# A layer with a 32-expert mixture streamed from HBM: expert order, a ninth gate/up buffer, an in-place residual, down chunks in 8 KB pieces

## The chip, the cores and the metric

The kernel runs on one core of one Trainium2 chip. The metric is the device time of one execution in microseconds (us). Engine names in the profile: PE is the matrix engine, PEld its weight loads, DVE the vector engine, ACT the scalar engine, POOL the GpSimd engine, SP the sync engine, on whose queue nearly all loads are issued.

## What is computed

One layer on 256 tokens of 1024 channels, everything in float32. First a token-mixing part (a convolution branch and a spatial gating branch, merged and projected). Then layer norm, and a mixture of 32 experts in which every token uses the four experts with the highest router logits. An expert is a gated unit of width 1024:

```python
gate, up = jnp.split(xb @ w_gu[e] + b_gu[e], 2, axis=-1)
gate = jnp.minimum(gate, SWIGLU_LIMIT)
up = jnp.clip(up, -SWIGLU_LIMIT, SWIGLU_LIMIT)
act = (up + 1) * (gate * jax.nn.sigmoid(SWIGLU_ALPHA * gate))
return act @ w_dn[e] + b_dn[e]
```

Its results are weighted by the softmax of the four logits, summed per token, multiplied by a gate vector g2 (made from the conditioning input), added to 2^(1/4) times the residual, and normed. The weights `w_gu` are 8 MiB per expert and `w_dn` 4 MiB.

## The kernel before

The token mixer comes first; its weights pass through five tiles `raw` of 1 MiB and are split into high and low parts in tiles `hi` and `lo`. Routing follows: the top four of each token, the tokens per expert, and the experts sorted by their number of tokens. Expert 0 is always worked first, since its weights can be loaded before the routing is known; the other places of the list `KINDS` (line 32) are filled by rank.

The expert stage is a list of 30 jobs, one expert each, written out by hand. The kind of a job says how many tokens it has room for (`CAP`): W 192, A 128, B 64, C 32. A "wide" job (W, A) feeds PE 128 columns of tokens; B puts two groups of 64 columns of the PE array side by side and C four groups of 32, so that a chunk of weights needs fewer passes. W is an A and a B at once. A float32 product appears in the profile as two passes (two MATMUL instructions). Experts with more tokens than their place has room for would be finished by tail jobs at the end, each under a condition; with these inputs none is run.

A job needs 12 chunks of weights of 1 MiB: 8 gate/up chunks (128 rows of `w_gu`, 8 KB per partition) and 4 down chunks (256 rows of `w_dn`; partition p holds rows p and 128 + p, two pieces of 4 KB). Loads are issued on SP's queue in the order in which the buffers come round: gate/up chunks through `N_G` = 7 buffers, the five `raw` tiles and two of a pool `rawx`, and down chunks through `N_D` = 4 buffers of `rawx`. The pool `rawx` lies where `hi` and `lo` were. `next_gu` and `next_dn` issue the next load right after the product that read the buffer's last content; a load waits on the queue until the buffer is free, and what is behind it on the queue waits too.

The order on PE, from the main loop (line 1371 on): the gate/up products of job j, then the down products of job j - 1. Smaller pieces of work are put between the chunks from a list `waiting`, one step per chunk (`tick`, `begin`): the gather of the next batch of jobs' tokens (`BATCHES`, at most 256 columns each, line 948), the transposes of the gate/up result (line 1208), the activation on DVE and ACT (lines 1176 to 1196), the slot weights (lines 1104, 1105), and the scatter of finished outputs into the result `y` (lines 1334, 1342). `until` runs steps from the list until a condition holds. An output tile `ob` (`N_OB` = 3) is taken by a wide job or by two narrow ones together, and given back at its scatter.

The result `y` has a tile of its own in the pool `a8` (seven slots of 8 KB per partition, shared with the gathered inputs `S`, the down bias, W's extra tile `wx` and the routed tokens); `start_units` sets it to the weighted down bias times g2 plus the scaled residual `x1`.

Column c of the gate/up result sits in block c // 128, so that the transposed activations of a block lie on 128 partitions, in the order in which the rows of `w_dn` are loaded.

Of the kernel before, what the change touches and what calls it, by code (L numbers as in the profile page):

```python
# [9 lines left out]
F32 = mybir.dt.float32  # L10
# [4 lines left out]
ALU = mybir.AluOpType  # L15
# [13 lines left out]

KINDS = ("B", "B", "A", "C", "C", "W", "C", "C", "A", "C", "C", "B", "B", "A", "C", "C", "A", "C", "C",
         "B", "B", "B", "B", "C", "C", "A", "C", "C", "C", "C")
CAP = {"W": 192, "A": 128, "B": 64, "C": 32}
RANK0 = {"W": 1, "A": 2, "B": 7, "C": 14}
BATCHES = ((0, 1, 2), (3, 4, 5), (6, 7, 8, 9, 10), (11, 12, 13), (14, 15, 16, 17, 18), (19, 20, 21, 22),
           (23, 24, 25, 26, 27), (28, 29))
NSTATIC = len(KINDS)
COLS = [j + sum(k == "W" for k in KINDS[:j]) for j in range(NSTATIC)]
NV = COLS[-1] + 1  # L40
# [19 lines left out]
NAT_O = (0,)  # L60
AHEAD = 2
N_RAW, N_HI, N_LO = 5, 9, 6
N_G, N_D = 7, 4
N_OB = 3
K_NORM = 5
C_M1 = 2.26
END0 = True
# [8 lines left out]
def kernel(ctx, tc, a, out):  # L76
# [114 lines left out]
    def load_gu(col, k, raw):  # L191
# [4 lines left out]
        sp.dma_start(raw, src)  # L196
        return raw

    def load_dn(col, ci, raw):
        if col == 0:  # L200
            src = a["w_dn"][0, 0, ci * 256:(ci + 1) * 256].rearrange("(k p) c -> p k c", p=P)
        else:
            src = a["w_dn"][0, ds(expert_reg(col), 1), ci * 256:(ci + 1) * 256].rearrange("o (k p) c -> p (o k) c", p=P)
        sp.dma_start(raw.rearrange("p (k c) -> p k c", k=2), src)
        return raw

    def next_gu():
        m = count["xg"]
        count["xg"] += 1
        if m < NSTATIC * KC:  # L210
            raw = raw_x("xg", N_G - N_RAW) if m % N_G < N_G - N_RAW else raw_tile()
            ring_g.append(load_gu(COLS[m // KC], m % KC, raw))

    def next_dn():
# [499 lines left out]
    rawx.append(ctx.enter_context(tc.tile_pool(name="rawx", bufs=1, side="right")))  # L714
    bgr = yap.tile([E, 2 * D], F32, name="bgr", tag="ya")
    sp.dma_start(bgr, a["b_gu"][0])
    for i in range(N_G):
        next_gu()
    for i in range(N_D):
        next_dn()  # L720
# [181 lines left out]
    for t in range(NT):  # L902
        ve.tensor_tensor(P1[:, t], pj[:, t * 64:t * 64 + NV], first_tok, op=ALU.add)
    g2_step(100)

    mix.close()
    tmp = ctx.enter_context(tc.tile_pool(name="tmp", bufs=2))
# [103 lines left out]
    base_q = const.tile([P, NTAIL], F32, name="base_q")  # L1011
    tgt_q = const.tile([P, NTAIL], F32, name="tgt_q")
    P1q = const.tile([P, NT, NTAIL], F32, name="P1q")
    bcols = const.tile([P, 2 * KC, NJOB], F32, name="bcols")

    def tail_unit():

# [39 lines left out]
                                        op0=ALU.add, op1=ALU.subtract)  # L1057
        return [counts, starts, places]

    def bias_unit(h):  # L1060

        box = []

        def mm():
            box.append(MS())
            for c in range(KC):
                pe.matmul(box[0][:, c * 64:c * 64 + NJOB], lhsT=bgr[:, (h * KC + c) * P:(h * KC + c + 1) * P],
                          rhs=J[:, 0:NJOB], start=True, stop=True)

        def out_():  # L1070
            ve.tensor_scalar(bcols[:, h * KC:(h + 1) * KC], box[0].rearrange("p (c j) -> p c j", c=KC)[:, :, 0:NJOB],
                             float(h), None, op0=ALU.add)
        return [mm, out_]

    def weight_unit():
# [17 lines left out]

    bdn = A8([E, D], name="bdn")
    gp.dma_start(bdn, a["b_dn"][0])
    y = A8([P, NT, D], name="y")

    def slot_weights(key, lhs_r, lhs_f, target, store):

# [74 lines left out]
    def swiglu_in(gv, uv, bg, bu, shape):  # L1174
        r = "p (c s) -> p c s" if len(shape) == 3 else "p (c h s) -> p c h s"
        kw = {"c": shape[1]} if len(shape) == 3 else {"c": shape[1], "h": shape[2]}
        n = 1
        for x in shape[1:]:
            n *= x
        gt = tmp.tile([P, 512], F32, name=nm("gt"), tag="gt", bufs=2)[:, 0:n]  # L1180
        ut = tmp.tile([P, 512], F32, name=nm("ut"), tag="ut", bufs=1)[:, 0:n]
        ve.tensor_tensor(gt.rearrange(r, **kw), gv, bg.to_broadcast(shape), op=ALU.add)  # L1182
        ve.tensor_scalar(gt, gt, 7.0, None, op0=ALU.min)
        sc.activation(gt, gt, AF.Silu, scale=SW_A)
        ve.tensor_tensor(ut.rearrange(r, **kw), uv, bu.to_broadcast(shape), op=ALU.add)
        ve.tensor_scalar(ut, ut, 8.0, -6.0, op0=ALU.min, op1=ALU.max)
        return gt.rearrange(r, **kw), ut.rearrange(r, **kw)

    def act_units(job):

        us = []
        col = job.col
        job.left = {"W": 4, "A": 2, "B": 2, "C": 1}[job.kind]

        def done(dst, gu):
# [9 lines left out]

        def transposes(ps, g, blocks):
            for i, c in enumerate(blocks):
                pe.transpose(ps[:, i * P:(i + 1) * P], g[:, c * P:(c + 1) * P], ident)  # L1208

        def bias(part, hh):  # L1210
            k0 = part * KC + hh * 4
# [137 lines left out]
    def start_units():  # L1349

        def unit(t, n):
            box = []

            def mm():
                box.append(MS())
                pe.matmul(box[0], lhsT=combT[:, t * P:(t + 1) * P], rhs=bdn[:, n * 512:(n + 1) * 512],
                          start=True, stop=True)
            ns = slice(n * 512, (n + 1) * 512)

            def out_():  # L1360
                ve.tensor_tensor(y[:, t, ns], box[0], g2c[:, ns], op=ALU.mult)
                ve.scalar_tensor_tensor(y[:, t, ns], x1[:, t, ns], ALPHA, y[:, t, ns], op0=ALU.mult, op1=ALU.add)
            return [mm, out_]
        return [unit(t, n) for t in range(NT) for n in range(2)]

# [70 lines left out]
    def tail_job(q):  # L1436
# [4 lines left out]
        for kk in range(KC // 2):  # L1441
            ps = MS()
            gather_mm(ps, St, kk, oht, P)
            gather_out(St, ps, kk, P)
        gu_open(job)
        for k in range(KC):
            gu_mm(job, k, load_gu(job.col, k, raw_tile()))
# [56 lines left out]
```

## Time and profile before

| what | value |
|---|---|
| three runs, lowest, median, highest | 1271.09, 1273.22, 1273.25 us |
| profiled execution, its span | 1268.86 us, 1267.0 us |
| PE busy | 1123.8 us (89%) |
| PEld busy | 548.3 us (43%) |
| DVE busy | 484.7 us (38%) |
| ACT busy | 205.7 us (16%) |
| read from HBM, mean rate over the span | 446.92 MB, 354 GB/s |
| gate/up loads | 240 of 1 MiB |
| down loads | 120 of 1 MiB |
| mean granted clock of TensorE | 0.954 |

The page divides the span into 40 slices and gives for each the busy share of the engines and the rate of the transfers. The ends of matrix instructions are modelled, so a busy PE is not one at its peak, and two passes that follow each other overlap in the record: the difference of two starts is the better measure of what a pass takes. A wait on SP's queue names what the next load waited for.

### The profile page before, as it was taken

Reading aid. Unit: us, or ns where it says so; the run is one execution under the profiler, and the core shown is the slowest. Engines: PE = TensorE matmul, PEld = TensorE weight load, DVE = VectorE, ACT = ScalarE, POOL = GpSimd, SP = SyncE. Lnnn points to the kernel's source line nnn. Section 1 sums busy time; section 2 is a strip of 40 time slices with the busy share of each in tenths; the row PEclk is TensorE's granted clock in tenths of the full one; section 3 lists DMA queues with packets and bytes.
Section 4 is the critical chain, followed back from the end, with each engine's and each line's share of the span. In section 5 each row is a group of like instructions: output and inputs, shape, how many; then the busy total and the mean of one; then the engine's idle time right before and its main releaser. Section 6 shows DMA issues by size and latency. Waiting matters only on the chain. (4 is left out here: it accounts for less than half of the span.)

```text
span 1267.0 us, 14367 instructions
## 1 busy us (share of the span) xinstructions
PE 1123.8 (89%) x5454; PEld 548.3 (43%) x5454; DVE 484.7 (38%) x926; ACT 205.7 (16%) x344; POOL 55.5 (4%) x185
## 2 busy tenths in 40 slices
PE   1999999998999989999997999899888986998672
PEld 1998898876434334324331343334222321332110
DVE  6799999976321410321222113121121211132124
ACT  1533234533202001000110020011000100011000
POOL 6000000000200001000010010000000000000000
PEclk9999999999999999999998999899889988999676
DMA  9984346685897998999999999999999999999993
GB/s 367 368 334 134 116 151 223 231 306 204 349 418 293 383 418 330 375 399 404 377 417 417 417 403 404 416 417 416 416 417 417 416 417 418 417 417 417 417 414 111
DMA packets 84312, 449.13 MB, mean 354 GB/s; under 512 B 7377, under 2 KB 7417, under 8 KB 51424
## 3 DMA queue, kind: packets, MB, share of 16 engines
q1 hardware_dynamic: 82672, 443.84, 87.8%
q0 software_dynamic: 1552, 4.15, 0.9%
q8 instruction: 50, 0.82, 0.3%
q14 instruction: 38, 0.31, 0.1%
HBM read 446.92 MB, written 1.05 MB: 354 GB/s over the span
## 5 line engine op out<-in xcount | busy, mean ns | idle before, releaser
L1138 PE MATMUL big<-raw,S 128*32 128x512 f32 (+1 forms) x1600 | 279.0, 631 | 30.3 <-DMA raw<-in_w_gu_dram 30.3
L1149 PE MATMUL big<-raw,S 128*128 128x512 f32 x384 | 172.2, 602 | 0.0
L1314 DVE TENSOR_TENSOR ob<-big,g2c 64x512 f32<-64x512 f32 x48 | 33.0, 688 | 361.8 <-PE big L1289 253.1
L1138 PEld LDWEIGHTS big<-raw,S 128*32 128x32 f32 (+1 forms) x1600 | 63.3, 122 | 202.7 <-issue 128.8
L1149 PEld LDWEIGHTS big<-raw,S 128*128 128x128 f32 x384 | 71.9, 192 | 90.4 <-issue 89.3
L1289 PE MATMUL big<-raw,aT 128*32 128x512 f32 x512 | 75.9, 706 | 30.5 <-DMA raw<-in_w_dn_dram 29.2
L516 DVE SCALAR_TENSOR_TENSOR sg<-ya,par,sg 128x256 f32<-128x256 f32 x240 | 100.0, 470 | 0.6
L1280 PE MATMUL big<-raw,aT 128*128 128x512 f32 x192 | 87.0, 601 | 0.9 <-DMA raw<-in_w_dn_dram 0.9
L426 PE MATMUL big<-hT,raw 128*128 128x256 f32 x384 | 85.5, 379 | 0.0
L1342 PE MATMUL ms<-ob,ohT 128*128 128x512 f32 x144 | 76.8, 640 | 5.9 <-DVE gt L1182 3.2
L1334 DVE TENSOR_TENSOR y<-y,ms 128x512 f32<-128x512 f32 x72 | 48.9, 685 | 81.8 <-PE ms L1342 81.7
L426 PEld LDWEIGHTS big<-hT,raw 128*128 128x128 f32 x384 | 71.9, 190 | 9.5 <-issue 0.5
L1138 PE MATMUL big<-raw,aT 128*64 128x512 f32 x256 | 65.1, 621 | 4.2 <-DMA raw<-in_w_dn_dram 4.1
L147 DVE TENSOR_TENSOR lo<-raw,hi 128x1024 fp32r<-128x1024 f32 x46 | 55.2, 1216 | 9.5 <-ACT hi L146 6.4
L1172 ACT COPY g<-big 128x512 f32<-128x512 f32 x16 | 9.4, 585 | 302.1 <-PE big L1138 302.1
L1280 PEld LDWEIGHTS big<-raw,aT 128*128 128x128 f32 x192 | 35.2, 190 | 52.4 <-issue 50.6
L146 ACT CAST hi<-raw 128x1024 fp32r<-128x1024 f32 x46 | 46.3, 1051 | 59.1 <-DMA raw<-in_w_in_dram 17.3
L430 PE MATMUL big<-hThi,lo 128*128 128x256 f32 x192 | 55.0, 288 | 0.8 <-DVE lo L147 0.8
L428 PE MATMUL big<-hThi,hi 128*128 128x256 f32 x192 | 55.7, 291 | 0.0
L429 PE MATMUL big<-hTlo,hi 128*128 128x256 f32 x192 | 55.0, 287 | 0.1
L1289 PEld LDWEIGHTS big<-raw,aT 128*32 128x32 f32 x512 | 13.9, 118 | 87.5 <-DMA raw<-in_w_dn_dram 59.3
L1182 DVE TENSOR_TENSOR gt<-ms,bcols 128x256 f32<-128x256 f32 (+1 forms) x46 | 22.6, 491 | 75.0 <-PE ms L1208 75.0
(327 smaller groups left out, 1185.5 us busy)
## 6 DMA issues: line engine op xcount, KB each, us to landing
raw<-in_w_gu_dram SPq DMA_DIRECT2D x240, 1024.0 KB, 17.2
raw<-in_w_dn_dram SPq DMA_DIRECT2D x120, 1024.0 KB, 16.6
raw<-in_w_mod_dram SPq DMA_DIRECT2D x24, 1024.0 KB, 7.6
raw<-in_w_in_dram SPq DMA_DIRECT2D x24, 1024.0 KB, 7.1
raw<-in_w_b_dram SPq DMA_DIRECT2D x4, 1024.0 KB, 5.0
raw<-in_w_a_dram SPq DMA_DIRECT2D x4, 1024.0 KB, 5.0
raw<-in_w_out_dram SPq DMA_DIRECT2D x4, 1024.0 KB, 9.0
x<-in_x_dram SPq DMA_DIRECT2D x1, 1024.0 KB, 8.3
```

The source lines that it names most:

```text
L147: ve.tensor_tensor(c.lo[q], src, f(c.hi[q]), op=ALU.subtract)
L426: pe.matmul(o, lhsT=ck.raw[:, k2 * D + n * P:k2 * D + (n + 1) * P], rhs=af[:, k], start=b0, stop=b1)
L428: pe.matmul(o, lhsT=ck.hi[k2][:, s], rhs=ahi[:, k], start=b0, stop=False)
L429: pe.matmul(o, lhsT=ck.hi[k2][:, s], rhs=alo[:, k], start=False, stop=False)
L430: pe.matmul(o, lhsT=ck.lo[k2][:, s], rhs=ahi[:, k], start=False, stop=b1)
L516: ve.scalar_tensor_tensor(cT[:, n], ya[:, n, t:t + T], bcol(n, t), cT[:, n], op0=ALU.mult, op1=ALU.add)
L1138: pe.matmul(out_[q * n:(q + 1) * n], lhsT=S, rhs=raw[:, w0(q):w0(q) + 512], start=first_, stop=last_)
L1149: pe.matmul(job.ps[h][:, n * 512:(n + 1) * 512], lhsT=S[:, k, 0:P], rhs=raw[:, h * D + n * 512:h * D + (n + 1) * 512], start=f0, stop=f1)
L1280: pe.matmul(job.pd[0][:, n * 512:(n + 1) * 512], lhsT=job.aT[:, k, 0:P], rhs=raw[:, k2 * D + n * 512:k2 * D + (n + 1) * 512], start=f0, st ...
L1289: pe.matmul(job.pd[0][q * 32:(q + 1) * 32, 0:512], lhsT=job.aT[:, k, 0:32], rhs=raw[:, k2 * D + h * 512:k2 * D + (h + 1) * 512], start=ci ...
L1334: ve.tensor_tensor(yy, yy, box[0], op=ALU.add)
L1342: pe.matmul(box[0], lhsT=w()[r, t * P:(t + 1) * P], rhs=o(n)[r], start=i == 0, stop=i == len(parts_) - 1)
```

## The change

- `KINDS` has the same 30 jobs in another order: W goes from the sixth place to the twenty-third, the first A from the third to the fifth, behind B B C C. `BATCHES` is cut anew to fit (still at most 256 columns a batch).
- `N_G` goes from 7 to 9. Of nine buffers in turn, the first five are `raw` tiles, the next three come from `rawx`, and the ninth from the pool `a8`. Before routing, the eight gate/up chunks of expert 0 are asked for; the ninth load, the second job's first, is issued after the routing result.
- The residual grows in place: `y` is the tile `x1` itself. `start_units` puts the bias product into a scratch tile and adds it to the scaled residual in `x1`.
- Down chunks: partition p now holds rows 2p and 2p + 1 of the 256, which lie together in memory: one piece of 8 KB. The transposed activations have to come in that order too, so block c of the gate/up result, and of the gate/up bias, is now every second column of a stretch of 256 (`chans`).
- Other sizes: two output tiles instead of three, one scratch tile `gt` instead of two, and bias columns for the 31 columns of the list and one tail job, which is filled when a tail job runs.

```diff
-KINDS = ("B", "B", "A", "C", "C", "W", "C", "C", "A", "C", "C", "B", "B", "A", "C", "C", "A", "C", "C",
-         "B", "B", "B", "B", "C", "C", "A", "C", "C", "C", "C")
+KINDS = ("B", "B", "C", "C", "A", "C", "C", "B", "B", "A", "C", "C", "A", "B", "B", "B", "B", "C", "C",
+         "A", "C", "C", "W", "C", "C", "A", "C", "C", "C", "C")
...
-BATCHES = ((0, 1, 2), (3, 4, 5), (6, 7, 8, 9, 10), (11, 12, 13), (14, 15, 16, 17, 18), (19, 20, 21, 22),
-           (23, 24, 25, 26, 27), (28, 29))
+BATCHES = ((0, 1, 2, 3), (4, 5, 6, 7), (8, 9, 10, 11), (12, 13, 14), (15, 16, 17, 18), (19, 20, 21), (22, 23, 24),
+           (25, 26, 27, 28, 29))
...
-N_G, N_D = 7, 4
-N_OB = 3
+N_G, N_D = 9, 4
+N_OB = 2
...
+    def chans(c):
+        c0 = c // 2 * 256 + c % 2
+        return slice(c0, c0 + 255, 2)
...
-            src = a["w_dn"][0, ds(expert_reg(col), 1), ci * 256:(ci + 1) * 256].rearrange("o (k p) c -> p (o k) c", p=P)
-        sp.dma_start(raw.rearrange("p (k c) -> p k c", k=2), src)
+            src = a["w_dn"][0, ds(expert_reg(col), 1), ci * 256:(ci + 1) * 256].rearrange("o (p k) c -> p (o k c)", k=2)
+        sp.dma_start(raw, src)
...
-            raw = raw_x("xg", N_G - N_RAW) if m % N_G < N_G - N_RAW else raw_tile()
+            i = m % N_G
+            raw = raw_tile() if i < N_RAW else raw_x("xg", N_G - 1 - N_RAW) if i < N_G - 1 else A8([P, 2 * D], name="raw")
...
-    for i in range(N_G):
+    for i in range(min(N_G, KC)):
         next_gu()
...
     g2_step(100)
+    for i in range(KC, N_G):
+        next_gu()
...
-    bcols = const.tile([P, 2 * KC, NJOB], F32, name="bcols")
+    bcols = const.tile([P, 2 * KC, NV + 1], F32, name="bcols")
...
-                pe.matmul(box[0][:, c * 64:c * 64 + NJOB], lhsT=bgr[:, (h * KC + c) * P:(h * KC + c + 1) * P],
-                          rhs=J[:, 0:NJOB], start=True, stop=True)
+                pe.matmul(box[0][:, c * 64:c * 64 + w], lhsT=src[:, chans(h * KC + c)],
+                          rhs=J[:, c0:c0 + w], start=True, stop=True)
...
-    y = A8([P, NT, D], name="y")
+    y = x1
...
-        gt = tmp.tile([P, 512], F32, name=nm("gt"), tag="gt", bufs=2)[:, 0:n]
+        gt = tmp.tile([P, 512], F32, name=nm("gt"), tag="gt", bufs=1)[:, 0:n]
...
-                pe.transpose(ps[:, i * P:(i + 1) * P], g[:, c * P:(c + 1) * P], ident)
+                pe.transpose(ps[:, i * P:(i + 1) * P], g[:, chans(c)], ident)
...
-                ve.tensor_tensor(y[:, t, ns], box[0], g2c[:, ns], op=ALU.mult)
-                ve.scalar_tensor_tensor(y[:, t, ns], x1[:, t, ns], ALPHA, y[:, t, ns], op0=ALU.mult, op1=ALU.add)
+                gb = tmp.tile([P, 512], F32, name=nm("gt"), tag="gt", bufs=1)
+                ve.tensor_tensor(gb, box[0], g2c[:, ns], op=ALU.mult)
+                ve.scalar_tensor_tensor(y[:, t, ns], y[:, t, ns], ALPHA, gb, op0=ALU.mult, op1=ALU.add)
```

## Rows read from the trace of the kernel before

**Rows 1.** The page's part 2, 40 slices of 31.7 us each, the rate of all transfers.

```profile
GB/s 367 368 334 134 116 151 223 231 306 204 349 418 293 383 418 330 375 399 404 377 417 417 417 403 404 416 417 416 416 417 417 416 417 418 417 417 417 417 414 111
```

**Rows 2.** Windows, expert stage: us; busy PE, PEld, DVE, ACT, POOL; PEclk; DMA; GB/s.

```profile
322.00:1240.00 918.00, 831.62 (x3685) 298.33 (x3683) 198.87 (x414) 90.28 (x166) 22.05 (x59) 0.95 0.99 402
```

**Rows 3.** The same view, gate/up chunks alone, then down chunks alone.

```profile
1198.00:1210.00 12.00, 10.30 (x35) 2.88 (x28) 4.62 (x10) 1.00 (x2) 0.00 (x0) 0.60 1.02 421
1216.50:1226.30 9.80, 6.44 (x34) 0.77 (x32) 0.00 (x0) 0.00 (x0) 0.00 (x0) 0.65 1.02 410
```

**Rows 4.** The same view in windows of 20 us, four of ten.

```profile
380.00:400.00 20.00, 20.00 (x78) 10.84 (x77) 1.77 (x5) 4.43 (x9) 1.78 (x4) 1.00 0.93 358
400.00:420.00 20.00, 20.00 (x97) 7.23 (x98) 8.64 (x15) 3.67 (x5) 1.26 (x4) 1.00 0.70 279
...
500.00:520.00 20.00, 20.00 (x132) 7.53 (x129) 8.71 (x18) 5.10 (x7) 0.30 (x2) 1.00 0.70 260
...
780.00:800.00 20.00, 19.65 (x97) 6.40 (x99) 5.62 (x11) 1.00 (x2) 0.00 (x0) 1.00 0.99 396
```

**Rows 5.** Waits of the sync queue, 322 to 1240 us: total us, times, longest.

```profile
SPq L196 <- PE big L1138: 255.9, 112, 13.5
```

**Rows 6.** Gate/up loads (L196), 340 to 1220 us: issue to landing.

```profile
DMA to landing us min/median/max: 4.7/17.5/21.2
```

**Rows 7.** PE in order of time, 455 to 545 us: start, us, operation, count.

```profile
460.38 3.60 PE L1149 MATMUL big<-raw,S 128*128 128x512 f32 x8
463.91 1.94 PE L1138 MATMUL big<-raw,S 128*64 128x512 f32 x8
465.78 3.70 PE L1149 MATMUL big<-raw,S 128*128 128x512 f32 x8
...
488.36 0.50 PE L948 MATMUL ms<-oh,hnhi 128*128 128x256 f32 x2
...
489.41 3.60 PE L1149 MATMUL big<-raw,S 128*128 128x512 f32 x8
...
507.50 3.64 PE L1289 MATMUL big<-raw,aT 128*32 128x512 f32 x32
...
512.95 1.92 PE L1138 MATMUL big<-raw,S 128*32 128x512 f32 x16
514.81 1.09 PE L1208 MATMUL ms<-ident,g 128*128 128x128 f32 x8
...
519.76 1.04 PE L1342 MATMUL ms<-ob,ohT 128*128 128x512 f32 x2
520.73 1.07 PE L1138 MATMUL big<-raw,S 128*32 128x512 f32 x8
...
523.88 1.88 PE L1280 MATMUL big<-raw,aT 128*128 128x512 f32 x4
...
526.70 1.98 PE L1280 MATMUL big<-raw,aT 128*128 128x512 f32 x4
```

**Rows 8.** PE in order of time, 405 to 445 us: A's down chunks.

```profile
423.82 13.14 PE L1280 MATMUL big<-raw,aT 128*128 128x512 f32 x30
```

**Rows 9.** PE's groups by line and shape, 322 to 1241 us (busy us, mean ns).

```profile
L1208 PE MATMUL ms<-ident,g 128*128 128x128 f32 x224 | 36.7, 293 | 15.7 <-ACT g L1172 7.6 <-ACT g L1170 7.0 <-DVE gt L1182 1.0
```

**Rows 10.** The sync queue in order of time, 255 to 345 us.

```profile
274.91 20.96 SPq L196 DMA_DIRECT2D raw<-in_w_gu_dram  x4
295.90 0.43 SPq L204 DMA_DIRECT2D raw<-in_w_dn_dram  x1
302.80 0.33 SPq L196 DMA_DIRECT2D raw<-in_w_gu_dram  x1
303.17 0.43 SPq L204 DMA_DIRECT2D raw<-in_w_dn_dram  x1
311.18 6.96 SPq L196 DMA_DIRECT2D raw<-in_w_gu_dram  x2
```

**Rows 11.** All engines in order of time, 1228 to 1270 us.

```profile
1240.87 1.06 PE L1289 MATMUL big<-raw,aT 128*32 128x512 f32 x8 [1.10 <-DMA raw<-in_w_dn_dram]
```

More of the change, by code (lines that the diff above doesn't have):

```diff
@@ L197, in load_gu @@
         return raw
+    def chans(c):
+        c0 = c // 2 * 256 + c % 2
+        return slice(c0, c0 + 255, 2)
     def load_dn(col, ci, raw):
         if col == 0:
-            src = a["w_dn"][0, 0, ci * 256:(ci + 1) * 256].rearrange("(k p) c -> p k c", p=P)
+            src = a["w_dn"][0, 0, ci * 256:(ci + 1) * 256].rearrange("(p k) c -> p (k c)", k=2)
         else:
-            src = a["w_dn"][0, ds(expert_reg(col), 1), ci * 256:(ci + 1) * 256].rearrange("o (k p) c -> p (o k) c", p=P)
-        sp.dma_start(raw.rearrange("p (k c) -> p k c", k=2), src)
+            src = a["w_dn"][0, ds(expert_reg(col), 1), ci * 256:(ci + 1) * 256].rearrange("o (p k) c -> p (o k c)", k=2)
+        sp.dma_start(raw, src)
         return raw
@@ L1058, in tail_unit, with bias_unit @@
         return [counts, starts, places]
-    def bias_unit(h):
+    def bias_unit(h, src=bgr, c0=0, dst=0, n=NV, w=NV):
         box = []
@@ L1066, in mm @@
             for c in range(KC):
-                pe.matmul(box[0][:, c * 64:c * 64 + NJOB], lhsT=bgr[:, (h * KC + c) * P:(h * KC + c + 1) * P],
-                          rhs=J[:, 0:NJOB], start=True, stop=True)
+                pe.matmul(box[0][:, c * 64:c * 64 + w], lhsT=src[:, chans(h * KC + c)],
+                          rhs=J[:, c0:c0 + w], start=True, stop=True)
         def out_():
-            ve.tensor_scalar(bcols[:, h * KC:(h + 1) * KC], box[0].rearrange("p (c j) -> p c j", c=KC)[:, :, 0:NJOB],
-                             float(h), None, op0=ALU.add)
+            ve.tensor_scalar(bcols[:, h * KC:(h + 1) * KC, dst:dst + n],
+                             box[0].rearrange("p (c j) -> p c j", c=KC)[:, :, 0:n], float(h), None, op0=ALU.add)
         return [mm, out_]
@@ L1191, in act_units @@
         us = []
-        col = job.col
+        col = NV if job.tail else job.col
         job.left = {"W": 4, "A": 2, "B": 2, "C": 1}[job.kind]
@@ L1444, in tail_job @@
             gather_out(St, ps, kk, P)
+        br_ = raw_tile()[:E]
+        sp.dma_start(br_, a["b_gu"][0])
+        waiting.extend(bias_unit(h, br_, job.col, NV, 1, 8) for h in range(2))
+        flush()
         gu_open(job)
```

## The prediction

> **What bounds the kernel now.** I read the page's slices first [rows 1]. From the twelfth slice on the transfers run at 417 GB/s nearly everywhere; the slices well below that (293, 330, 375) all lie in the first half of the expert stage. In the slices before it the token mixer runs, at 116 to 368 GB/s, and the transfers are not the limit. So in the expert stage (322 us to 1240 us) the bound is the weight stream: 30 experts of 12 chunks of 1 MiB. The window over that stage [rows 2] shows 402 GB/s over 918 us with PE busy for 832 us of it.
>
> Next, what the stream could do. In a stretch where only gate/up chunks are moving the rate is 421 GB/s, in one with only down chunks 410 GB/s [rows 3]. 1,048,576 bytes divided by these is 2.49 us and 2.56 us per chunk. Two gate/up chunks to one down chunk give 417.4 GB/s, so the stage lost (1 - 402/417.4) x 918 = 33.9 us to holes in the stream.
>
> Then where the holes are. From 360 us on ten windows of 20 us lie below 400 GB/s, of which [rows 4] shows four, the first and the last among them; each window's hole is (417.4 - rate)/417.4 x 20 us. Those from 380 to 440 us hold 11.9 us (2.8 and 6.6 of it in the two shown), those from 480 to 520 us 9.8 us (7.5 in 500:520), the other five, up to 780:800, 7.7 us. Together 29.4 us; the remaining 4.5 us are single late transfers and the start. In the windows of the holes PE is busy without a pause: there PE is the limit.
>
> Last, why. The sync queue issues loads in order and each needs a free buffer; its longest waits in sum are for PE to finish reading [rows 5]. A load takes between 4.7 us and 21.2 us to land [rows 6]: 4.7 us when the stream is empty (2.2 us of start beside the 2.49), and about 20 us, eight chunks, when PE is the one that waits.
>
> **What each expert asks of PE.** Pitches are read as differences of starts. W's gate chunk is a wide part of 3.5 us (460.38 to 463.91) and a 64-row part of 1.87 us (463.91 to 465.78) [rows 7]. So A costs 3.5 us per gate chunk (28 us) and the same per down chunk (13.1 us for 30 of the 32 passes [rows 8], 14 us), C 0.93 us per gate chunk (16 passes from 512.95 to 514.81) and 3.64 us for all its down chunks [rows 7], B 1.87 us for each of 12 chunks, W 5.4 us per gate chunk and 2.82 us for each half of a down chunk (523.88 to 526.70; 22.6 us). Each part's scatter is four products of about 1.0 us (519.76 to 520.73); two narrow experts share one. A transpose takes 0.13 us (8 in 1.09 us from 514.81 on). Slot weights add some 0.3 us to a narrow expert, 0.7 us per wide part, and a batch's gather 4 us (four units like 488.36 to 489.41). Sums: A 28 + 14 + 2 + 4 + 1 = 49 us, B 22.4 + 1 + 2 + 0.3 = 26, C 7.4 + 3.6 + 0.5 + 2 + 0.3 = 14, W 43.2 + 22.6 + 3 + 8 + 1.4 = 78. The 12 chunks of an expert take the stream 30.2 us. So A puts PE 19 us behind and W 48 us; B gives back 4 and C 16. In total 5 x 49 + 8 x 26 + 16 x 14 + 78 + 8 x 4 = 787 us: PE has time enough, only not where it is needed.
>
> **The order.** Before, the stage opens B B A: at its start every buffer is full, two B's give back 8 us, A takes 19, and the stream stands still from 380 us on. Then C C W: PE starts W with the stream about 20 us deep in queued loads; W's gate stage runs 47.1 us (460.38 to 507.50 [rows 7]); the stream lives on 20 + 8 x 2.49 = 39.9 us, so it is dry for 7.2 us, plus one restart of 2.2 us: 9.4 us, and the windows gave 9.8 us. The rule holds, so I apply it to the new order. B B C C gives back 8 + 32 us, more than the full buffers (11 to 13 chunks, 27 to 32 us), so the first A starts with PE waiting for data: its 28 us and some 3 us of transposes and scatter are less than 39.9, no hole. Each A C C asks 49 + 28 + 4 = 81 us of PE against 90 of the stream, so the later A's start the same way. W C C asks 78 + 28 + 4 = 110 us against 90.
>
> **Nine buffers.** Two more gate/up buffers are 5 us of stream. W's gate stage loses the gather it now shares (three units, 2.8 us, as W is no longer the last of its batch) and gains four transposes: about 45 us against 39.9 + 5 = 44.9, no hole to speak of. Behind W C C PE owes 20 us, and A's gate stage adds 31 - 20 = 11: 31 us against 13 chunks less the two being read, 27 us. That leaves 4 us and a restart of 2.2: 6 us of holes, all at the A after W. Bounds: none, if the C's run at their pace with full clock, and 18 us, what A and W together have now. With the 4.5 us of stray ones: 10.5 us against 33.9, **-23.4 us**.
>
> **Down chunks in 8 KB pieces.** The rows of a gate/up chunk are 8 KB already, and the move makes the two layouts equal, so I take the gate/up rate [rows 3]: 119 chunks x (2.557 - 2.491) us = **-7.9 us**; the other end is 0. The Trainium skill's "DMA: Bandwidth & Descriptors" (Specifications) gives 512 B as the least piece for line rate; by that rule 4 KB pieces lose nothing and this term is 0, against a difference of 2.7% in the rows.
>
> **The strided transposes this needs.** The same channels now sit at stride two in the copied gate tile, for the 224 + 8 transposes at L1208 and the bias products. No row shows PE reading at a stride. Lower end: nothing. Upper end: by the nearest row, the contiguous transpose [rows 7, 9], a doubling is 232 x 0.13 = 30 us more PE work, 1 us per expert, of which only that in W, the A after it and the C's between them (some 5 us) is uncovered; elsewhere PE waits for data anyway. I take 0. The Trainium skill's "SBUF — State Buffer" (Door 1: The DMA port swizzle) says that fp32 reads may skip within a 16-byte line at no cost, which would be this case; no run here shows it.
>
> **The start.** Before routing only expert 0 can be loaded. Before, four gate/up loads went out from 274.91 to 295.87 us, a down load at 295.90, and then one or two each time a chunk of the gate vector was used up; the ninth went out at about 317.8 us (the second of the pair from 311.18 on) and, with 4.7 us in an empty stream, landed at about 322.5 [rows 10]. Now there are eight gate/up loads instead of seven ahead of the four down loads, the raw tiles are filled first, and the ninth comes after the routing result. I expect the third new buffer to take the place of the first down load in the queue at 295 us: again nine landed by 322.5 us, **0 us**. Bounds: if the raw tiles block the queue until their chunks are free (302.80, 311.18, 317.8), four fewer have landed, +10 us; if all of the space opens at 295 us, two more, -5 us. The queue behind a blocked load is only other loads; PE starts expert 0 at 320 us in either case, as its gather sets that.
>
> **What costs nothing.** The ninth buffer lives in the seven slots shared with the gathered inputs, W's extra tile and the down bias; the separate result tile leaves that pool as the residual takes its place, so at most seven are live, as before. It is loaded when its own last reader is done. Cover gone, 26 loads would each pay up to a restart of 2.2 us, 57 us. Two output tiles instead of three: an output waits for the scatter one expert earlier, which is in PE's order before it; forced early it is the same work, 0 to 1 us per A. One gate scratch tile: its uses follow one another on DVE already. The in-place residual has as many instructions as before. The tail code isn't run. After the last landing nothing changes: the last down product at 1240.87 us [rows 11] is followed by 26.1 us of scatter, branches, norm and output.
>
> **Sum.** The profiled span is 1267.0 us, the execution 1268.86. -23.4 - 7.9 = -31.3 us: 1237.6 us for that execution. The median of the runs shown lies 4.36 us above it, so 1241.9 us, **1242 us**.
>
> **Rivals.** (1) *The pieces bring nothing* (the lower rate of the down stretches comes from something else in them): 1250 us. For it: nothing in the rows but that only two kinds of stretches are compared. (2) *The raw tiles block the queue at the start*: 1252 us. For it: these loads did hold up down loads behind them [rows 10]. (3) *The two buffers don't reach the stream*, since no more than eight chunks are in flight (21.2 us at most [rows 6]): W's hole stays at 5 + 2.2 us, 1249 us. Against it: a landed chunk that waits for PE is also a lead. (4) *Nothing is left at the A after W and more lands early*: 6 + 5 us less, 1231 us; with one of them about 1236 us. (5) Slower: *the strided reads make PE the bound.* Place: L1208. At five times the price PE's 787 us grow by 232 x 0.52 = 121 to 908 us; its waits for copies, first data and uneven order (832 busy and 86 idle of the 918 us, of which some 40 remain) bring that to 948 us, 30 us over the 918 us of now: 1273 + 30 = 1303 us. It decides from about four times the price on (787 + 40 + 91 = 918); at three times there is still a gain. For it: only that no row shows such a read.
>
> **How the numbers follow.** Forecast 0.54; (1) 0.12, (2) 0.10, (3) 0.10, (4) 0.08, (5) 0.04, and 0.02 for no change by several of these at once. Forecast's own spread is holes of 4.5 to 22.5 us: 1236 to 1254 us. Adding (1) to (3) in part, one with another and a doubled transpose (+6): up to 1260; (4) sets the lower end: 1231 to 1260 us. A measurement of this kernel can't tell less than 0.2% from no change. Every case but the last two is faster by more: 0.94 faster, 0.02 same, 0.04 slower.
>
> **What would show it.** The windows from 380 to 520 us at 417 GB/s or more, those with only down chunks at 421; a dip only some 740 us into the stage, at the A behind W; nine chunks landed at 322.5 us; the last down product about 1210 us; L1208's mean near 0.29 us as now [rows 9]. Wrong if the dips come with every ninth load, if transposes are several times longer, or if the first window after 322 us is starved.

## The result, and the profile after

The changed kernel takes 1256.24 us (median; 1253.1 to 1257.74, 4 runs) against 1272.15 us in the same session: ratio 0.988, interval 0.986 to 0.9896. That is faster by 1.2%, clear of the noise, inside the range, and 14 us above the predicted 1242. The profiled execution went from 1268.86 to 1257.14 us where 1237.6 was forecast: it is 19.5 us short.

Two rows of PE divide this. The first product of an expert started at 320.30 us before and at 326.98 us after; the last down chunk's product, which follows the last landing, at 1240.87 [rows 11] and 1229.13 us. So the start lost 6.7 us, the stage between them went from 920.6 to 902.1 us (31.3 less was forecast, 18.4 came: 12.9 short), and the tail, from that product to the end of the span, is 25.9 us (26.1 before). After, PE in order of time at both ends:

```profile
326.98 1.94 PE L1147 MATMUL big<-raw,S 128*64 128x512 f32 x8
...
1229.13 1.06 PE L1298 MATMUL big<-raw,aT 128*32 128x512 f32 x8 [1.07 <-DMA raw<-in_w_dn_dram]
```

The slices of the page after, beside [rows 1], each 31.4 us. From the twelfth to the thirty-first they lie at 418 to 420 GB/s; then come four of 396, 305, 390 and, two further on, 352. The holes of the first half are gone; there are new ones around W and the A behind it, which now stand late.

```profile
GB/s 365 366 317 165 102 132 237 180 330 196 311 420 419 419 420 419 418 420 420 420 420 419 419 420 419 419 419 419 420 420 419 396 305 390 417 352 419 418 406 119
```

Windows after, beside [rows 2, 4]: the stage, three places that were dips before, and W's gate stage and the A's behind it.

```profile
329.00:1229.00 900.00, 823.40 (x3683) 302.76 (x3681) 200.63 (x414) 90.82 (x166) 21.84 (x57) 0.96 1.00 410
380.00:400.00 20.00, 17.59 (x115) 6.69 (x114) 5.41 (x13) 1.80 (x4) 0.28 (x1) 1.00 1.01 421
400.00:420.00 20.00, 11.34 (x75) 1.83 (x73) 0.00 (x0) 2.42 (x5) 0.00 (x0) 0.82 1.01 419
500.00:520.00 20.00, 15.84 (x104) 5.46 (x98) 3.69 (x8) 2.93 (x6) 0.00 (x0) 1.00 1.01 419
980.00:1000.00 20.00, 20.00 (x62) 6.85 (x60) 0.48 (x1) 0.38 (x1) 0.28 (x1) 1.00 0.97 402
1000.00:1020.00 20.00, 20.00 (x82) 6.83 (x84) 0.00 (x0) 3.04 (x3) 0.00 (x0) 1.00 0.61 216
1100.00:1120.00 20.00, 20.00 (x82) 8.19 (x80) 0.00 (x0) 2.02 (x2) 0.00 (x0) 1.00 0.83 311
```

In the quiet windows PE is busy for 11 to 18 of 20 us and the transfers run without a gap: there the stream is the limit. In the last three PE is busy throughout, and the stream falls to 402, 216 and 311 GB/s. The sync queue's waits from 322 to 1240 us say the same: its largest are now for the transfers themselves. Those of gate/up loads for the narrow products fell from 255.9 us [rows 5] to 132.7, those for the wide parts of W and A from 114.0 to 50.8. Before, then after:

```profile
SPq L196 <- PE big L1149: 114.0, 34, 12.0
```

```profile
SPq L196 <- DMA raw<-in_w_gu_dram: 143.1, 76, 2.9
SPq L196 <- PE big L1147: 132.7, 72, 10.6
...
SPq L196 <- PE big L1158: 50.8, 17, 5.1
```

Holes can also be counted by the landings of the 360 loads: the time between two landings, less 2.491 us a chunk, or 2.557 us for a down chunk of before; whatever is over 0.3 us, behind the ninth landing. So counted they were 35.1 us before and are 23.4 us after.

### The profile page after: what moved, and what is told of

Read it like the earlier page. It is cut to its first block, busy times and chain, and to the rows that moved or that the text cites. A ratio compares the mean times of both kernels' runs of the same rounds, so it can differ in the third digit from the quotient of the medians.

```text
span 1255.0 us, 14491 instructions
## 1 busy us (share of the span) xinstructions
PE 1122.0 (89%) x5454; PEld 558.4 (44%) x5454; DVE 486.9 (39%) x928; ACT 206.1 (16%) x344; POOL 51.4 (4%) x183
## 5 line engine op out<-in xcount | busy, mean ns | idle before, releaser
L1147 PE MATMUL big<-raw,S 128*32 128x512 f32 (+1 forms) x1600 | 275.0, 623 | 22.4 <-DMA raw<-in_w_gu_dram 22.4
L1343 DVE TENSOR_TENSOR x<-x,ms 128x512 f32<-128x512 f32 x72 | 49.3, 686 | 188.8 <-PE ms L1351 188.5
L1298 PE MATMUL big<-raw,aT 128*32 128x512 f32 x512 | 82.0, 730 | 28.8 <-DMA raw<-in_w_dn_dram 24.5
L1193 ACT ACTIVATE gt<-gt 128x256 f32<-128x256 f32 (+1 forms) x46 | 21.7, 472 | 334.7 <-DVE gt L1192 334.7
L1147 PE MATMUL big<-raw,aT 128*64 128x512 f32 x256 | 57.9, 596 | 0.7 <-DMA raw<-in_w_dn_dram 0.7
L1217 PEld LDWEIGHTS ms<-ident,g 128*128 128x128 f32 x224 | 32.2, 208 | 57.0 <-issue 23.4
L1217 PE MATMUL ms<-ident,g 128*128 128x128 f32 x224 | 40.5, 314 | 18.7 <-ACT g L1181 7.3
L1289 PEld LDWEIGHTS big<-raw,aT 128*128 128x128 f32 x192 | 35.8, 190 | 45.1 <-issue 44.9
```

The lines of the kernel that those rows point to most:

```text
L1147: pe.matmul(out_[q * n:(q + 1) * n], lhsT=S, rhs=raw[:, w0(q):w0(q) + 512], start=first_, stop=last_)
L1217: pe.transpose(ps[:, i * P:(i + 1) * P], g[:, chans(c)], ident)
L1289: pe.matmul(job.pd[0][:, n * 512:(n + 1) * 512], lhsT=job.aT[:, k, 0:P], rhs=raw[:, k2 * D + n * 512:k2 * D + (n + 1) * 512], start=f0, st ...
L1298: pe.matmul(job.pd[0][q * 32:(q + 1) * 32, 0:512], lhsT=job.aT[:, k, 0:32], rhs=raw[:, k2 * D + h * 512:k2 * D + (h + 1) * 512], start=ci ...
```

## The experiments

The stage is the last down chunk's start less the first expert product's, from each run's profile; the time is the median. Differences are in us against the kernel before in the same session. A profile is of one execution, which can lie some microseconds off the median: that of the pieces alone took 1271.81 us, 4.2 above it, that of the order alone 1264.26, 3.3 below, that of the late A with 192 bytes 1241.21, 3.0 below.

| kernel | first product | stage | median | to before | ratio, interval |
|---|---|---|---|---|---|
| before | 320.3 | 920.6 | 1272.15 | | |
| changed | 327.0 | 902.1 | 1256.24 | -15.9 | 0.9878 [0.986, 0.9896] |
| order alone | 321.2 | 915.1 | 1267.58 | -4.2 | 0.9968 [0.9946, 0.9991] |
| pieces alone | 324.1 | 919.7 | 1267.62 | -4.1 | 0.996 [0.9939, 0.9981] |
| all but the order | 326.5 | 913.2 | 1267.22 | -4.5 | 0.9963 [0.9944, 0.9983] |
| changed, again | 326.8 | 900.8 | 1255.71 | -16.0 | 0.9859 [0.983, 0.9889] |
| late A | 325.2 | 895.7 | 1250.11 | -22.5 | 0.9826 [0.9803, 0.985] |
| seven buffers | 325.5 | 917.0 | 1271.71 | -0.9 | 0.9995 [0.9976, 1.0013] |
| seven, tiles moved back | 321.3 | 915.0 | 1265.64 | -6.9 | 0.9955 [0.9935, 0.9975] |
| 4 KB pieces | 325.4 | 909.4 | 1263.40 | -9.2 | 0.9926 [0.9899, 0.9953] |
| late A, batches recut | 325.1 | 901.8 | 1258.58 | -12.6 | 0.989 [0.9866, 0.9915] |
| late A, 192 bytes | 320.0 | 893.0 | 1244.26 | -26.9 | 0.9773 [0.9748, 0.9797] |
| before, 64 bytes | 324.5 | 922.8 | 1277.33 | +6.1 | 1.004 [1.0021, 1.0058] |
| late A, 64 bytes | 324.7 | 894.8 | 1247.31 | -23.9 | 0.9804 [0.9774, 0.9834] |

**The parts one at a time.** The first runs take the change apart. The order alone, in the kernel before (KINDS and BATCHES of the diff, nothing else):

> The kernel before with the new order of jobs and batches alone (seven buffers, 4 KB pieces, own result tile). Holes theory (what PE cannot do in the time the buffers bridge is lost to the stream, wherever it falls): the dips from 380 to 520 us go, W's gate stage at about 965 us leaves a hole of some 16 us (50.8 us of PE work against 20 + 8 x 2.49 = 39.9 us, and two restarts of 2.2), the A behind it about 8: 24 + strays 4.5 against 34, so 5 to 10 us faster than before, about 1264 us. Rival (the order alone is the whole gain): 16 us faster, 1256 us. Rival (the late start belongs to the change): first expert product at 320 us here, 327 us in the full change.

The pieces alone, in the kernel before (chans(), load_dn, the bias products and the transposes of the diff, nothing else):

> The kernel before with down chunks in 8 KB pieces and the strided transposes alone. Holes theory: 2.49 us instead of 2.56 us a down chunk, 7.9 us less stream, of which about 2 us come back as longer holes where PE is behind: 5 to 7 us faster, about 1266 us; a window with only down chunks reads 421 GB/s. Rival (strided reads cost as much as they bring): no change, 1272 us, transposes at twice their 0.13 us.

All but the order: the changed kernel with KINDS and BATCHES of before:

> The changed kernel with the order and batches of before: nine buffers, 8 KB pieces, in-place residual. Holes theory: the pieces' 6 us and two chunks more (5 us each at the A in the third place, at W and at the A's behind it): 14 to 21 us faster than before, 1251 to 1258 us, as fast as the full change or faster. Rival (the order is the whole gain): 6 us faster, 1266 us. If the ninth buffer or the third xg buffer makes the start late, the first expert product is at 327 us here too; if the start only differs between executions, it may be anywhere from 320 to 327 us.

And the changed kernel once more:

> The changed kernel unchanged, profiled again. If its late start (first expert product at 326.98 us against 320.3 us before, with the same code ahead of it) is the change's, it is within 1 us of 327 again; if it differs from execution to execution, it lies elsewhere between 319 and 328 us. The holes at W and the A behind it are there again, 16 us within 1.

Order and pieces bring some 4 us each by themselves, nine buffers with pieces in the old order 4.5, and all of them 16. So they don't add up. (Nine buffers alone were not run, and the start takes part of it: 326.5 us in all but the order, 324.1 with the pieces.) The traces show why. With seven buffers and the old order PE is what the stream waits for: with pieces alone the down chunks land 0.066 us earlier each and the holes grow from 35.1 to 42.8 us, so that in the profiled execution what is saved on the way is given back at the next wide expert. With the order alone the early holes close, and those at W and A reappear from 1000 us on (29.7 us in all). Pieces alone, then the order alone:

```profile
400.00:420.00 20.00, 20.00 (x96) 8.38 (x94) 3.62 (x7) 4.96 (x8) 3.04 (x7) 1.00 0.62 242
```

```profile
1000.00:1020.00 20.00, 20.00 (x114) 7.46 (x116) 4.97 (x9) 3.67 (x4) 0.00 (x0) 1.00 0.78 295
```

Two forecasts of these runs failed. A hole of 16 us was expected at W with the order alone; the landings give 4.7 to 5.7 us, since W's gate stage took 44.0 us there (967.08 to 1011.07) and not the 50.8 of the changed kernel. And 14 to 21 us were expected of all but the order; 4.5 came, with holes of 34.3 us against the 42.8 of the pieces alone, and 13.0 of them at W (landings from 507.9 to 520.5 us), whose gate stage took 52.3 us there (463.33 to 515.63): PE's order puts three units of a gather and three down chunks of the expert ahead into it.

**Seven buffers in the new order.**

```
-N_G, N_D = 9, 4
+N_G, N_D = 7, 4
```

> The changed kernel with seven gate/up buffers instead of nine (five raw tiles, one extra, one of the shared slots); order, 8 KB pieces and in-place residual as changed. Two questions. The stream: theory, two buffers are 5 us of lead at W and at the A behind it, each: the holes grow by 8 to 12 us over the changed kernel's 23 us; rival, the order alone has closed what they could close: 0 to 2 us. The start, where the kernels with nine buffers reached the first expert product at 326.5 to 327 us and before at 320.3: theory a, the late start comes with the buffers (loads in flight, slots taken from others): back to 320 to 321 us. Theory b, it comes with where the mixer's tiles lie (the smaller bias tile moves the pools above it), which this kernel shares with the changed one: 326 to 327 us. Time: by theory and a 1258 to 1262 us, by theory and b 1264 to 1268 us, by rival and b 1256 to 1258 us.

The theory's direction held and its size did not: the stage is 15 to 16 us longer than with nine, not 8 to 12. The lead of two chunks also counts away from W and the A behind it: among the B's behind the third A a window that runs at 419 GB/s with nine buffers is half empty with seven. Seven buffers:

```profile
760.00:780.00 20.00, 18.89 (x78) 6.47 (x78) 7.15 (x15) 3.63 (x8) 3.61 (x9) 1.00 0.55 217
```

At W itself the two buffers change little: with seven the landings give 6.7 us there, with nine 6.6. For with seven, PE has the gather and the scatter done ahead of W, and W's gate stage takes 44.0 us, the size that the prediction had given it:

```profile
978.20 3.70 PE L1158 MATMUL big<-raw,S 128*128 128x512 f32 x8
...
1022.19 3.64 PE L1298 MATMUL big<-raw,aT 128*32 128x512 f32 x32
```

And order with pieces is not better than the order alone (915 to 917 against 915.1 us of stage): without the lead the pieces are worth nothing that these runs can tell. The start, 325.5 us, did not return to 320 with the buffers; theory b was left.

**4 KB pieces.** In the changed kernel load_dn, chans() and the transposes of before:

```
-        c0 = c // 2 * 256 + c % 2
-        return slice(c0, c0 + 255, 2)
+        return slice(c * P, (c + 1) * P)
...
```

> The changed kernel with down chunks in 4 KB pieces again and unstrided transposes; order, nine buffers and in-place residual as changed. Theory: the pieces set the rate of down chunks: 2.56 us each instead of 2.49, about 119 x 0.066 = 7.9 us less whatever holes take up, so 1261 to 1264 us; the transposes' mean falls from 0.314 to 0.293 us and PE's weight loads at them from 208 to 141 ns, worth 0 to 2 us. Rival: with the new order the stream has slack beside PE, the pieces are hidden: 1256 us. Rival on the other side: the strided transposes cost more than the pieces give: below 1254 us.

1263.4 us, as the theory said; the pieces, with the strided transposes that they need, are worth 7.2 to 7.7 us of the median beside the two runs of the changed kernel, 7 to 9 us of the stage. The window from 420 to 960 us, without a hole worth the name in either, first of the changed kernel, then with 4 KB:

```profile
420.00:960.00 540.00, 495.78 (x2145) 187.61 (x2145) 116.97 (x231) 54.91 (x101) 17.38 (x45) 0.97 1.01 420
```

```profile
420.00:960.00 540.00, 495.17 (x2133) 185.00 (x2137) 116.73 (x231) 54.87 (x101) 17.38 (x45) 0.96 1.02 416
```

The strided transposes, first of the changed kernel (busy us, mean ns: products, then their weight loads), then unstrided:

```profile
L1217 PE MATMUL ms<-ident,g 128*128 128x128 f32 x224 | 40.5, 314 | 18.7 <-ACT g L1181 7.3 <-DVE gt L1191 6.0 <-ACT g L1179 4.5
L1217 PEld LDWEIGHTS ms<-ident,g 128*128 128x128 f32 x224 | 32.2, 208 | 57.0 <-issue 23.4 <-ACT g L1181 18.0 <-ACT g L1179 8.0
```

```profile
L1216 PE MATMUL ms<-ident,g 128*128 128x128 f32 x224 | 35.0, 287 | 18.9 <-ACT g L1180 7.3 <-DVE gt L1190 6.0 <-ACT g L1178 4.5
L1216 PEld LDWEIGHTS ms<-ident,g 128*128 128x128 f32 x224 | 24.9, 143 | 56.4 <-issue 22.5 <-ACT g L1180 18.0 <-ACT g L1178 8.0
```

A strided weight load takes 208 ns against 143, a transpose 314 against 287: 5.5 us of PE over the stage. What of it reaches the time was not told apart from what the pieces bring.

**The A behind W, later.**

```
-         "A", "C", "C", "W", "C", "C", "A", "C", "C", "C", "C")
+         "A", "C", "C", "W", "C", "C", "C", "C", "A", "C", "C")
```

> The changed kernel with its last A moved behind two more C's (W C C C C A C C in place of W C C A C C C C). Theory: the holes at 1010 to 1120 us are PE's debt from W (78 us asked against 30 us delivered, only two C's to pay it back before A asks 49 us more). With four C's between, the debt is paid back: the dip at A (311 GB/s at 1100:1120 in the changed kernel, about 7.6 us) shrinks to 1 to 2 us, the dip at W (216 GB/s at 1000:1020) stays, and the time is 5 to 7 us under the changed kernel's: 1249 to 1251 us. Rival a: A now stands so late that its 49 us on PE reach the end, the work after the last landing grows from 26 us by 4 to 8 us and eats the gain: about 1256 us. Rival b: the dips at 1010 to 1120 us are not PE's but the transfers' own at that time: both stay, 1256 us.

1250.1 us, as expected, with the tail unchanged (25.7 us). The window in which the A stood, 311 GB/s in the changed kernel, now:

```profile
1100.00:1120.00 20.00, 15.31 (x79) 3.99 (x79) 3.05 (x5) 0.97 (x2) 0.00 (x0) 0.86 1.02 420
```

By landings the holes from 1100 to 1140 us went from 5.9 to 0.6 us, those at W stayed (8.0 and 7.5 us, of which 1.4 and 1.3 come six loads later). So the dip at the A was PE's debt from W, and two narrow experts pay it.

**W's gate stage, emptied.** In the late-A kernel:

```
-BATCHES = ((0, 1, 2, 3), (4, 5, 6, 7), (8, 9, 10, 11), (12, 13, 14), (15, 16, 17, 18), (19, 20, 21), (22, 23, 24),
-           (25, 26, 27, 28, 29))
+BATCHES = ((0, 1, 2, 3), (4, 5, 6, 7), (8, 9, 10, 11), (12, 13, 14), (15, 16, 17, 18), (19, 20), (21, 22, 23),
+           (24, 25, 26, 27, 28), (29,))
```

> The kernel with the late A, and its last batches cut anew: (19,20), (21,22,23), (24 to 28), (29) in place of (19,20,21), (22,23,24), (25 to 29), one batch more. W's batch is then gathered one expert earlier, and PE's order has neither its gather (two units, 2.3 us) nor the scatter of the A two experts before (3.6 us) nor the slot weights (0.7 us) inside W's gate stage. Theory: the hole at W is the excess of W's gate stage over the stream's lead (50.8 us against 45): the stage takes 44 to 45 us, the holes at W (6 to 7.5 us at landings 278 to 286 of the late-A kernel) shrink to 1 to 2 us; one more gather (4 us of PE) falls among narrow experts. Time 4 to 6 us under the late-A kernel's 1250: 1244 to 1246 us. Rival a: the moved work lands on PE just ahead of W, where it takes the same lead away: 1249 to 1250 us. Rival b: the hole at W is not PE's: 1250 us.

The forecast fell, and what it stood on did not come about: the gate stage took 48.7 us (964.03 to 1012.74), not 44 to 45. The gather and the scatter left it, but they now lie in the expert ahead, and three of that expert's down chunks, which had been done before W, came into W's stage instead. Its holes went from 7.5 to 6.5 us. So the work that was moved one expert forward pushed other work back into the stage (rival a, in its effect); what a stage of 44 us would give with nine buffers stays untested. PE with the batches recut, from W's first product to its gate's end; the lines between are W's products and those of the narrow expert's down chunks:

```profile
964.03 2.84 PE L1158 MATMUL big<-raw,S 128*128 128x512 f32 x6
966.81 1.06 PE L1298 MATMUL big<-raw,aT 128*32 128x512 f32 x8
...
1012.74 3.64 PE L1298 MATMUL big<-raw,aT 128*32 128x512 f32 x32
```

The time is 8.5 us worse, since the added batch is the last expert's alone and stands behind an A at the very end: a hole of 6.0 us before the last four landings, and a tail of 28.7 us.

```profile
1200.00:1220.00 20.00, 15.76 (x94) 4.36 (x97) 6.51 (x13) 1.77 (x4) 0.00 (x0) 0.99 0.67 273
```

**The late start.** The bias tile bcols of the change is 1216 bytes a partition smaller, and it lies below the pools of the mixer. The unused tile here puts them back where they were, with seven buffers:

```
     bcols = const.tile([P, 2 * KC, NV + 1], F32, name="bcols")
+    const.tile([P, 304], F32, name="pad")
```

> As the run with seven buffers, with an unused tile of 1216 bytes a partition beside the bias tile, so that the pools above it, the mixer's among them, lie where they lay in the kernel before. Theory (place of the mixer's tiles): in 55:83 us PE does 240 to 249 products as before instead of 235 to 236, the first expert product is at 320 to 321 us, 6 us earlier than without the pad if that is late. Rival (not the place): the same start as without the pad, whatever that is, within 1 us.

The theory held: 321.3 us in place of 325.5, and 1265.64 us in place of 1271.71. Nine buffers leave no room for 1216 bytes, so the late A got 192, the same place modulo 1024:

```
+    const.tile([P, 48], F32, name="pad")
```

> The kernel with the late A and an unused tile of 192 bytes a partition beside the bias tile. 1216 bytes, the whole shift of the mixer's tiles, brought 6 us with seven buffers; with nine there is no room for it, but 192 bytes bring the tiles to the same place modulo 1024. Theory a (what counts is where a tile lies within a block of up to 1 KB): the first expert product comes at 321 to 322 us as before, 4 us earlier, time 1244 to 1247 us. Theory b (what counts is the place itself, or the phase in which the mixer runs against its transfers): no change, 1249 to 1251 us.

First product at 320.0 us, 1244.26 us: theory a, and the fastest kernel of this case, 12 us under the changed one and 5.9 under the late A. To see it without any of the change, the kernel before got 64 bytes:

```
     bcols = const.tile([P, 2 * KC, NJOB], F32, name="bcols")
+    const.tile([P, 16], F32, name="pad")
```

> The kernel before with an unused tile of 64 bytes a partition beside the bias tile, and nothing of the change. The change's smaller bias tile moves the pools above it down by 1216 bytes, which is 64 bytes up modulo 128 and 256. Theory: the place of the mixer's tiles within a block of 128 or 256 bytes sets the mixer's pace; this kernel then has the changed kernel's start: 235 to 236 products in 55:83 us, first expert product at 325 to 327 us instead of 320, time 4 to 6 us over before's: 1275 to 1278 us. Rival a (a block of 512 or 1024 bytes counts, or the 192 bytes helped for another reason): start and time as before within 1 us, 1271 to 1273 us.

324.5 us and 1277.33 us: 64 bytes that nothing reads cost the kernel before 6 us (interval of the ratio 1.0021 to 1.0058). And the late A with 64:

> The kernel with the late A and an unused tile of 64 bytes a partition, where 192 bytes gave 1244.3 us and none 1250.1 us. The tiles then lie where they lay before modulo 128, but not modulo 256. If a block of up to 128 bytes counts: start at 320 us as with 192 bytes, 1243 to 1246 us. If a block of 256 bytes or more counts: start at 325 us, 1249 to 1251 us.

1247.3 us, between the two answers: the mixer's products are a third of the way back (240 in the window below, against 236 and 250), but the start is not (324.7 us). So the place within 128 bytes is not all that counts.

What the place does is seen in two views. The window from 55 to 83 us, deep in the mixer, PE busy all the time at full clock: 249 products before; 235 with 64 bytes more; 236 in the changed kernel; 250 with the late A and 192 bytes. They are the same products in the same order in all of them. Before, then the others as named:

```profile
55.00:83.00 28.00, 28.00 (x249) 28.00 (x249) 23.15 (x16) 10.70 (x16) 0.00 (x0) 1.00 0.94 361
```

```profile
55.00:83.00 28.00, 28.00 (x235) 28.00 (x235) 21.73 (x15) 10.82 (x16) 0.00 (x0) 1.00 0.93 352
```

```profile
55.00:83.00 28.00, 28.00 (x236) 28.00 (x235) 23.51 (x16) 10.71 (x16) 0.00 (x0) 1.00 0.92 348
```

```profile
55.00:83.00 28.00, 28.00 (x250) 28.00 (x249) 22.24 (x15) 10.71 (x16) 0.00 (x0) 1.00 0.95 364
```

And behind the mixer PE waits 3.24 us for the norm. In the three kernels with 249 or 250 products the clock then stays at 2.4 GHz; in all others but the order alone it falls for some microseconds to the lower level, 1.2 GHz (granted clock 0.89 to 0.94 in 295:325 against 1.00), though the wait is the same. The window, and the products behind the wait, before, then after:

```profile
295.00:325.00 30.00, 26.23 (x134) 15.28 (x134) 20.10 (x71) 7.74 (x14) 4.78 (x11) 1.00 0.77 290
298.27 1.06 PE L781 MATMUL ms<-ident,hn 128*128 128x128 f32 x8 [3.24 <-DVE hn L774]
299.17 3.60 PE L492 MATMUL big<-raw,condT 128*128 128x512 f32 x8
```

```profile
295.00:325.00 30.00, 26.05 (x117) 16.33 (x115) 18.86 (x61) 7.40 (x13) 1.90 (x6) 0.94 0.54 210
303.08 1.63 PE L788 MATMUL ms<-ident,hn 128*128 128x128 f32 x8 [3.24 <-DVE hn L781]
304.50 4.76 PE L499 MATMUL big<-raw,condT 128*128 128x512 f32 x8
```

From these transposes on to the first expert product pass 22.0 us before and 23.9 us after; the other 4.8 of the 6.7 us were lost ahead of them. Open is which tile's place it is and whether PE's reads or the transfers suffer first (in the window PE does 5 to 6% fewer products and the transfers run 3% slower), and why the order alone and the pieces alone, with no tile moved by their diffs, have 241 and 240 products there. So the place of the tiles moves the pace, by the three pairs of kernels that differ in an unused tile alone, but it is not the only thing that does. Open too is what decides on the clock: except for the changed kernel there is one profile of each.

## Why the prediction was right and where it failed

**What bounds it: right.** The stream, with holes where PE is behind. The runs fit: what closes a hole at PE or speeds up a chunk pays only where the other does not wait.

**The order, first half: right.** "B B C C gives back 8 + 32 us": the windows from 380 to 520 us hold 419 to 421 GB/s, against 260 to 358 in those shown of [rows 4]. The order alone does this too: its first hole over 0.5 us behind 350 us lands at 593.7 us.

**W's gate stage: the step that failed.** The prediction put it at "about 45 us against 39.9 + 5 = 44.9, no hole to speak of". It took 50.8 us (965.89 to 1016.67), and PE after shows with what:

```profile
964.23 1.72 PE L1298 MATMUL big<-raw,aT 128*32 128x512 f32 x8 [0.56 <-DMA raw<-in_w_dn_dram]
965.89 1.12 PE L1158 MATMUL big<-raw,S 128*128 128x512 f32 x2
966.45 0.80 PE L957 MATMUL ms<-oh,hnhi 128*128 128x256 f32 x2
...
968.51 0.40 PE L957 MATMUL ms<-oh,hnlo 128*128 128x256 f32 x2
968.75 1.02 PE L1158 MATMUL big<-raw,S 128*128 128x512 f32 x2
969.62 3.79 PE L1351 MATMUL ms<-ob,ohT 128*128 128x512 f32 x8
973.24 1.88 PE L1158 MATMUL big<-raw,S 128*128 128x512 f32 x4
...
1016.67 3.64 PE L1298 MATMUL big<-raw,aT 128*32 128x512 f32 x32
```

Two gather units of W's own batch (966.45 to 968.75: 2.3 us) and a scatter (969.62 to 973.24: 3.6 us) come after W's first two passes, where the prediction had them done. By the prediction's rule of lead and restart this makes 50.8 - 44.9 + 2.2 = 8.1 us; the landings give 6.6 us (1010.5 to 1021.6) and 1.4 us more six loads later (1037.9), 8.0 together, though that load went out 14 us before it landed, and whether its delay is W's is not shown. With seven buffers in the new order the rule gives 44.0 - 39.9 + 2.2 = 6.3 us against 6.7, with the batches recut 48.7 - 44.9 + 2.2 = 6.0 against 5.1 to 6.5. In the old order with nine buffers it fails: W's stage from 463.33 to 515.63 us would make 9.6 us, and it is 13.0. So in the new order the rule comes within 2 us, on a stage sized wrong. The recut batches show that the 5.9 us can't just be moved one expert forward. What has to be sized is all that PE's own order puts between W's first product and the end of its gate stage: gathers, scatters and a neighbour's down products too.

**The A behind W: right.** 6 us were forecast, the landings give 5.9, and it closed with the late A. That it fits to a tenth is luck: 4.5 us come with the A's gate stage (landings from 1105.3 to 1119.1 us), 1.4 us at 1137.9, behind it.

**Strays: too small.** 4.5 us were carried over; it is 9.5 us: 2.1 at the start, 1.6 behind W's down chunks, 1.2 at the last expert, and seven single late landings of 0.4 to 0.8 us. Each of these seven comes within 4 us behind a packet on one of the two queues that the page calls instruction (q8 and q14; for the landing at 901.8 us one of 8 KB at 900.3). Most of the 44 such packets from 340 to 1220 us are followed by no late landing, so this is a coincidence that no run tested. W 8.0 + A 5.9 + 9.5 = 23.4 us, against the 10.5 forecast: 12.9 us, the stage's miss.

**Nine buffers: right, and worth more than the prediction thought.** The rival that they don't reach the stream (1249) is refuted by the run with seven, 15.5 us slower. But the gain is not at W, where the prediction had put it: the hole there is as long with seven (6.7 against 6.6 us), with a gate stage that is 6.8 us shorter in that run. That the ninth, in the shared slots, costs nothing held too: its loads go out 1.8 us after the load before them in the mean of 25, those into the other eight 2.4 to 3.5 us.

**8 KB pieces: right.** -7.9 us were forecast, 7 to 9 measured, with nine buffers in the new order; in the old one or with seven, less or nothing. The rival of 1250 by pieces that bring nothing falls. The Trainium skill's "DMA: Bandwidth & Descriptors" (Specifications) gives 512 B as the least transfer for line rate, by which 4 KB would be as good as 8 KB. The windows of 420 and 416 GB/s, a third of whose chunks are down chunks, say it is not for this load.

**Strided transposes: nearly right.** 0 was taken and 30 us was the bound; it is 5.5 us of PE, a fifth of a doubling, and the slower rival (1303) falls. The Trainium skill's "SBUF — State Buffer" (Door 1: The DMA port swizzle) lets fp32 skip within a 16-byte line for free; the weight loads at 208 against 143 ns disagree.

**The start: failed, for a reason that no rival had.** 0 us was forecast, with bounds of +10 and -5; it was +6.7. The queue did not cause it. After, six gate/up loads go out before the first down load:

```profile
279.84 29.79 SPq L196 DMA_DIRECT2D raw<-in_w_gu_dram  x6
309.67 0.43 SPq L210 DMA_DIRECT2D raw<-in_w_dn_dram  x1
```

With the same queue and 192 bytes of padding the ninth chunk landed at 322.2 us, the forecast's 322.5, and the first product came at 320.0. The prediction did not cost the smaller bias tile at all: it treated the size of a tile as free.

**The sum.** By an estimate that takes each hole off the time in full, the profile would have read 1257.1 - 6.7 - 8.0 = 1242.4 us had the start stayed and W's stage been 45 us; the rest, 4.8 us over the forecast, is about the 5.0 us by which the strays were too small.

## What to carry to other kernels

When a stream feeds an engine through a ring, size the hole at a heavy stage by all the work that the engine's own order puts into that stage (gathers, scatters, a neighbour's products) against the lead in the ring, and add one restart. Parts that attack the same bound from both sides don't add up: here the order and the pieces bring 4 us each alone, nine buffers with the pieces 4.5, and all of them 16, so one that "does nothing" may only lack its partner. And whatever resizes a tile moves others: time the change with a few bytes of padding before judging its parts.

## What the runs showed of the hardware that was not expected

- An unused tile of 64 bytes a partition changes the pace of unrelated products: 249 to 235 in the same 28 us, and 6 us of a kernel's time (by the ratio's interval 3 to 7).
- The same wait of 3.24 us, after the same products, is followed by a clock drop in some of these kernels (8 passes in 4.76 us) and not in others (3.60 us). It did not fall where the mixer ran at its fast pace (249 and 250 products) and fell where it ran at the slow one (235 and 236); at 240 and 241 it did one or the other.
- An fp32 weight load at a stride of two elements takes 208 ns against 143; the product behind it 314 against 287.
- Chunks of 1 MiB in 4 KB pieces arrive 2.7% slower than in 8 KB pieces (2.557 against 2.491 us a chunk). Where the stream has few holes nearly all of it shows in the time (7.2 to 7.7 us), with the old order and seven buffers about half (4.1 us).
